# Two products of a recurrent scan, each split into two column halves of the matrix array

## The chip, the cores and the metric

The kernel runs on one core of one Trainium2 chip. A core has a matrix engine (TensorE, "PE" in the profile, with its weight loads shown apart as "PEld"), a vector engine (VectorE, DVE), a scalar engine (ScalarE, ACT), a general engine (GpSimd, POOL) and a queue engine that mostly starts transfers (SyncE, SP). The metric is the device time of one execution in microseconds, lower is better.

## The reference, cut to what matters

The kernel computes one layer of a bidirectional recurrent model on 128 context tokens and 2048 latent tokens of width 1024: a normalisation with modulation, one input projection, a mixer, an output projection. Half of the mixer's channels go through a gated short convolution. The other half, 8 heads of 64 channels, go through a delta-rule recurrence, once in each direction of time:

```
def step(S, inp):                       # S: (64 value x 64 key) per head
    r_t, w_t, k_t, v_t, kk_t, a_t = inp
    s_kk = einsum('bdhij,bdhj->bdhi', S, kk_t)
    S = S * w_t - s_kk x (kk_t * a_t) + v_t x k_t     # x: outer product
    return S, einsum('bdhij,bdhj->bdhi', S, r_t)
```

The states at the end of the context are an output as well, and the latent scans begin from cached states. All of it is in float32.

## The kernel before, in words

There are three phases: the input projection with everything that prepares the scan's operands (to about 1020 us of the span), the scan (about 1020 to 1590 us) and the output projection (from about 1525 us on, at first between the work of the scan).

The recurrence is cut into chunks of 64 tokens. A *unit* is one chunk of one pair of heads in one direction. A *stage* is two groups of 8 units, one group for each direction, and there are 17 stages (`stages`, L800 to L804). For each unit the kernel turns the 64 steps into a few matrix products:

- `partM` (L871) makes the products `psF` and `psG` (L892) and the transposes `psQ` (L885), three stages ahead of use.
- `partI` (L909) inverts small triangular blocks on GpSimd, and `partU` (L981) joins the 32 by 32 blocks of the inverse with products `psU` (L992) and `psW` (L999) on 32 by 32 tiles of the array.
- `partB` (L1011) applies the inverse, `psX` (L1018), which ScalarE copies into the operand tiles `stl` and `str`; and then makes the *operator* product `psE` (L1029), one for each unit and head: `g.lt` as weights (128 rows by 128 columns), `g.rt` as moving operand (128 rows by 128 columns). VectorE masks it into `E` (L1030).
- `partS` (L1034) walks through the 8 units of each group one after another. For each unit and head the *state* product `psS` (L1054) has `E` as weights (128 by 128) and `sv` as moving operand (128 rows by 64 columns: the state above, the values below). Its first 64 rows are the next state, which VectorE scales into the next unit's `sv` (L1067); its last 64 rows are the output (`outputs`, L1075), read by VectorE or ScalarE every fourth unit.

So the state product of a unit waits for VectorE's scaling after the one before it, in two chains (one for each direction), and all other products are there to be done between the links. The order in which the program emits the work is written out by hand (`ORDER`, L688, and the loop in `main`, L1172 to L1217). The framework's scheduler then orders the instructions of each engine by its own simulated timeline (L1409); the matrix engine's queue as it stands in the trace isn't the order of emission, but its own mixture of it. PSUM has 2 buffers for `partM` (`O.pm`), 2 for `psX`, `psE`, `psU`, `psW` and `psT` together (`O.p2`) and 4 for `psS` (`O.pS`).

A float32 product is two pairs of a weight load and a matmul in the profile: 17 stages with 2 groups of 16 products each are 544 products `psE`, and stand there as x1088; `psS` likewise.

Two products elsewhere are made on parts of the array already: `psU`/`psW`, which alternate between two 32 by 32 tiles, and `mod_rows` (L186 to L190), where four products, each with 128 rows by 32 columns of weights, write to the partitions 0, 32, 64 and 96 of one PSUM tile.

Of the kernel before, what the change touches and what calls it, by code (L numbers as in the profile page):

```python
# [690 lines left out]
def phase2(K):  # L691
    nc, tc, A, S = K.nc, K.tc, K.A, K.S
    V, G, P, T = nc.vector, nc.gpsimd, nc.scalar, nc.tensor
# [78 lines left out]
    def copy(k, dst, src, negate=False):  # L772
        if negate:
            if k in ON_DVE:
                V.tensor_scalar(dst, src, -1.0, None, ALU.mult)
            else:
                P.activation(dst, src, AF.Copy, scale=-1.0)  # L777
        else:
            (V.tensor_copy if k in ON_DVE else P.copy)(dst, src)  # L779
# [16 lines left out]
    def tl(shape, tag, b, pool=None, dt=F32):  # L796
        return (pool or O.l0).tile(shape, dt, tag=tag, name=f"{tag}_{K.u()}", bufs=b)
# [29 lines left out]
    H0, H1, FULL = slice(0, 64), slice(64, 128), slice(0, 128)  # L827
# [20 lines left out]
    def half(g, n):  # L848

        h = n if g.d == 0 else 1 - n  # L850
        return slice(h * 4, h * 4 + 4)
# [159 lines left out]
    def partB(s, st):  # L1011
        for n in range(2):
            for gi, g in enumerate(st.g):
                us = half(g, n)
                g.E.append(tl([128, 4, 2, 128], "E", 4))
                px = O.p2.tile([128, 4, 128], F32, tag="s", name=f"psX{s}_{gi}_{n}")
                for i in range(4):
                    T.matmul(px[:, i, :], B.zb[:, gi, us.start + i, :], g.F[:, us.start + i, :], start=True, stop=True)  # L1018
                for hd in range(2):
                    copy("x" if hd else "y", g.fs[64:128, :, hd, us], px[64 - hd * 64:128 - hd * 64].rearrange("p u (b t) -> p b u t", b=2), True)  # L1020
            yield
            for h2 in range(2):
                for gi, g in enumerate(st.g):
                    us = half(g, n)
                    k = (h2 if g.d == 0 else 1 - h2) * 2
                    pe = O.p2.tile([128, 2, 2, 128], F32, tag="s", name=f"psE{s}_{gi}_{n}{h2}")
                    for i in range(2):
                        for hd in range(2):
                            T.matmul(pe[:, i, hd, :].rearrange("p (b t) -> p b t", b=2), g.lt[:, :, hd, us.start + k + i].rearrange("p b t -> p (b t)"), g.rt[:, :, hd, us.start + k + i], start=True, stop=True)  # L1029
                    V.tensor_tensor(g.E[n][:, k:k + 2].rearrange("p a b c -> p (a b) c"), pe[:].rearrange("p a b c -> p (a b) c"),  # L1030
                                    B.msk[:, ME[g.d]].unsqueeze(1).broadcast_to((128, 4, 128)), ALU.mult)
                yield

    def partS(s, st, nxt):  # L1034

        sp = {}
        for i in range(8):
            for gi, g in enumerate(st.g):
                d = g.d
                ctx = g.blk is None  # L1040
                u = i % 4 * 2 + i // 4 if ctx else i
                u = u if d == 0 else 7 - u
                p, c = g.units[u]
                lastc = c == ((1 if d == 0 else 0) if ctx else (33 if d == 0 else 2))
                sv = g.sv
                n, k = (u // 4 if d == 0 else 1 - u // 4), u % 4

                m, q = (u % 2, u // 2) if ctx else (u // 4, u % 4)
                if i == 0 and not ctx and gi in held:
                    G.tensor_copy(sv[0:64, u], held.pop(gi)[:])  # L1050
                if i % 4 == 0:
                    sp[gi] = O.pS.tile([128, 4, 2, 64], F32, tag="S", name=f"psS{s}_{gi}_{i}")
                for hd in range(2):
                    T.matmul(sp[gi][:, q, hd, :], g.E[n][:, k, hd, :], sv[:, u, hd, :], start=True, stop=True)  # L1054
                if not (lastc and not ctx):
                    if ctx and lastc:
                        so = tl([64, 2, 64], "so", 2)
                        dst = so[:]
                    elif (not ctx) and i == 7:
                        if nxt.g[gi].blk is None:  # L1060
                            held[gi] = tl([64, 2, 64], "held", 2)
                            dst = held[gi][:]
                        else:
                            dst = nxt.g[gi].sv[0:64, 0 if d == 0 else 7]
                    else:
                        dst = sv[0:64, u + (1 if d == 0 else -1)]
                    r = V.tensor_tensor(dst, sp[gi][0:64, q], B.pc[0:64, d, 2 * p:2 * p + 2, c:c + 1].broadcast_to((64, 2, 64)), ALU.mult)  # L1067
                    O.scaled = r.ins
                    if ctx and lastc:
                        D(S["nst"][:, d, 2 * p:2 * p + 2, :], so[:])  # L1070
                if i % 4 == 3:
                    outputs(g.units[0][0], g.blk, m, sp[gi])
            yield

    def outputs(p, blk, m, ps):  # L1075

        y, there = ynew.setdefault((p, blk), (None, []))
        if y is None:
            y = tl([128, 4, 128], "y", 5)
            ynew[p, blk] = y, there  # L1080
        r = slice(m * 64, m * 64 + 64)
        src = ps[64:128].rearrange("p q h v -> p q (h v)")
        if m in there:
            V.tensor_tensor(y[r], src, y[r], ALU.add)
        else:
            copy("o", y[r], src)
        there.append(m)
        if len(there) == 4:
            ynew.pop((p, blk))
            pend.append(finish(p, blk, y))  # L1090
# [68 lines left out]
    def main():  # L1159
# [5 lines left out]
        sts[LA] = partL(LA)  # L1165
        run(partU(0, sts[0]))
        bb = partB(0, sts[0])
        next(W)
        for _ in range(3):
            next(bb)  # L1170
        tail = iter(())
        for s in range(NST):  # L1172
            st = sts.pop(s)
            more = s + 1 < NST
            W = partW(s + 1, sts[s + 1]) if more else iter(())
            uu = partU(s + 1, sts[s + 1]) if more else iter(())
            own, bb = bb, partB(s + 1, sts[s + 1]) if more else iter(())
            gens = dict(L=W, b=own, U=uu, B=bb)

# [23 lines left out]
            for i, _ in enumerate(partS(s, st, sts.get(s + 1))):  # L1203
                for _ in range((2, 2, 2, 1, 1, 0, 0, 0)[i]):
                    next(m, None)
                next(tail, None)
                if s < NST - 1:
                    emit(i + 1)
                for f in todo[:1] if s < NST - 3 else todo:
                    next(f, None)  # L1210
# [203 lines left out]
```

## Time and profile before

| what | value |
|---|---|
| median of 3 runs | 1759.63 us (1756.57, 1759.63, 1762.25) |
| span of the profiled execution, first to last instruction | 1752.9 us |
| what the median has beside that span | 6.7 us |
| PE busy / PEld busy | 1647.9 us (94%) / 1558.8 us (89%) |
| DVE / ACT / POOL busy | 1093.0 us (62%) / 870.1 us (50%) / 582.1 us (33%) |
| mean granted TensorE clock | 0.972 |

The profile gives the profiled execution's own time as this span; what stands beside it is start and end of the execution. A row of the timeline is "start us, duration us, engine, line, operation, out<-in, shapes, xcount", with the idle time before it in brackets; the shape of a matmul or weight load begins with rows\*columns of the weights. Successive instructions of a line are merged into one row. The end of a matmul is modelled: it lies some 0.17 us behind the moment at which the array could take the next, so the pace within a row of n matmuls is (duration of the row - duration of one) / (n - 1).

### The profile page before, as it was taken

The page shows a single profiled execution, that of the slowest core. Times are in us where ns is not written, and L with a number is a line of the kernel's source. Part 1 is how long each engine was busy: PE and PEld are TensorE (multiplying, and loading weights), DVE is VectorE, ACT ScalarE, POOL GpSimd, SP SyncE. Part 2 cuts the span into 40 slices and gives each one's busy share as a digit, 9 for nine tenths or more (in the row PEclk, how much of TensorE's full clock was granted, in tenths as well). Part 3 has the DMA queues.
Part 4 walks back from the last instruction along what each step waited for, and adds up shares of the span by engine and source line. Part 5 has one row for each costly group of instructions (what it writes and reads, how often), then busy time and mean ns, then how long its engine had stood idle before and what let it go on. Part 6 is the DMA issues. An engine that isn't in the chain of part 4 may idle for free. (4 is left out here: it accounts for less than half of the span.)

```text
span 1752.9 us, 33041 instructions
## 1 busy us (share of the span) xinstructions
PE 1647.9 (94%) x12400; PEld 1558.8 (89%) x12400; DVE 1093.0 (62%) x2092; ACT 870.1 (50%) x1719; POOL 582.1 (33%) x1089
## 2 busy tenths in 40 slices
PE   5999899998999999999998989999999999899998
PEld 2889898998999998999998979899999999787886
DVE  5875788866567766567764544475776666656333
ACT  4534455534143433334442367687788787633222
POOL 0011111111011101011120587777777778223221
PEclk9899999999999999999999998899999999999999
DMA  9797778785557646477666585587677875746442
GB/s 367 208 234 220 233 241 246 232 255 151 148 160 227 169 147 174 135 258 217 195 214 225 173 196 135 141 192 187 174 198 189 191 185 120 180 151 206 151 144 90
DMA packets 315825, 335.69 MB, mean 192 GB/s; under 512 B 166985, under 2 KB 263881, under 8 KB 301585
## 3 DMA queue, kind: packets, MB, share of 16 engines
q1 hardware_dynamic: 243360, 324.52, 62.6%
q10 hardware_dynamic: 70944, 4.60, 2.9%
q0 software_dynamic: 1360, 4.46, 0.7%
q8 instruction: 98, 1.61, 0.4%
q14 instruction: 63, 0.51, 0.1%
HBM read 221.42 MB, written 112.08 MB: 190 GB/s over the span
## 5 line engine op out<-in xcount | busy, mean ns | idle before, releaser
L934 POOL TENSOR_TENSOR zt<-zt,ztmp 128x30 f32<-128x30 f32 (+7 forms) x510 | 197.3, 387 | 39.3
L1054 PE MATMUL psS<-sv,E 128*128 128x64 f32 x1088 | 155.1, 277 | 1.0 <-DVE sv L1067 0.6
L1029 PE MATMUL psE<-str,stl 128*128 128x128 f32 x1088 | 144.1, 281 | 11.3 <-DVE E L1030 7.0
L1054 PEld LDWEIGHTS psS<-sv,E 128*128 128x128 f32 x1088 | 145.4, 200 | 3.3 <-DVE sv L1067 0.8
L1029 PEld LDWEIGHTS psE<-str,stl 128*128 128x128 f32 x1088 | 131.8, 194 | 14.1 <-DVE E L1030 7.9
L931 POOL TENSOR_TENSOR ztmp<-ab,zt 128x60 f32<-128x60 f32 (+7 forms) x255 | 130.8, 513 | 19.2
L1067 DVE TENSOR_TENSOR sv<-psS,pc 64x128 f32<-64x128 f32 x254 | 69.2, 277 | 92.9 <-PE psS L1054 92.2
L779 ACT COPY bd<-rr 64x512 f32<-64x512 f32 x136 | 84.0, 617 | 75.7 <-DMA rr<-scr_ops 23.3
L323 POOL TENSOR_TENSOR shk<-rawl 128x384 f32<-128x384 f32 (+1 forms) x24 | 20.7, 861 | 291.9 <-ACT rawl L319 291.9
L1030 DVE TENSOR_TENSOR E<-psE,msk 128x512 f32<-128x512 f32 x136 | 92.7, 684 | 33.0 <-PE psE L1029 32.3
L892 PE MATMUL psF<-rr,bd 128*128 128x128 f32 x544 | 80.0, 295 | 16.2 <-ACT Q L779 9.8
L892 PEld LDWEIGHTS psF<-rr,bd 128*128 128x128 f32 x544 | 70.7, 203 | 20.4 <-ACT Q L779 12.9
L1350 POOL TENSOR_TENSOR z<-z,x 128x512 f32<-128x512 f32 x32 | 43.6, 1364 | 126.6 <-DVE z L1346 105.9
L1018 PE MATMUL psX<-F,zb 128*128 128x128 f32 x544 | 78.2, 297 | 3.2 <-ACT zb L777 2.3
L197 POOL TENSOR_TENSOR hslb<-kd,hshb 128x384 fp32r<-128x384 f32 (+1 forms) x24 | 26.7, 1113 | 164.0 <-ACT hshb L196 143.5
L160 PE MATMUL mmc<-h,w 128*128 128x384 f32 (+1 forms) x192 | 67.9, 354 | 13.4 <-ACT q1r L321 9.8
L323 POOL TENSOR_TENSOR shv<-rawl 128x384 f32<-128x384 f32 (+1 forms) x24 | 25.4, 1060 | 153.4 <-ACT rawl L319 153.4
L892 PE MATMUL psG<-rr,bd 128*128 128x128 f32 x544 | 72.0, 280 | 4.4 <-DVE F L893 4.4
L1018 PEld LDWEIGHTS psX<-F,zb 128*128 128x128 f32 x544 | 71.6, 209 | 4.0 <-POOL zt L934 1.9
L892 PEld LDWEIGHTS psG<-rr,bd 128*128 128x128 f32 x544 | 65.7, 193 | 5.0 <-DVE F L893 4.8
L161 PE MATMUL mmc<-h,w 128*128 128x384 f32 (+1 forms) x192 | 66.1, 344 | 0.0
L162 PE MATMUL mmc<-h,w 128*128 128x384 f32 (+1 forms) x192 | 65.7, 342 | 0.0
(307 smaller groups left out, 5205.4 us busy)
## 6 DMA issues: line engine op xcount, KB each, us to landing
w<-scr_wsp SPq DMA_DIRECT2D x68, 1024.0 KB, 7.3
scr_wsp<-w SPq DMA_DIRECT2D x34, 1024.0 KB, 6.0
rr<-scr_ops SPq DMA_DIRECT2D x64, 512.0 KB, 4.6
scr_ops<-sp SPq DMA_DIRECT2D x160, 192.0 KB, 5.2
wr<-in_win SPq DMA_DIRECT2D x34, 512.0 KB, 6.3
ab<-scr_at SPq DMA_DIRECT2D x34, 256.0 KB, 4.2
x<-in_x SPq DMA_DIRECT2D x17, 512.0 KB, 3.8
wadas<-in_wada SPq DMA_DIRECT2D x8, 1024.0 KB, 13.0
```

The costliest lines, as they stand in the source:

```text
L160: T.matmul(ps[:, :n], w[:, 0, k], hh[:, 0, k, :n], start=k == 0, stop=False)
L161: T.matmul(ps[:, :n], w[:, 0, k], hh[:, 1, k, :n], start=False, stop=False)
L162: T.matmul(ps[:, :n], w[:, 1, k], hh[:, 0, k, :n], start=False, stop=k == 7)
L779: (V.tensor_copy if k in ON_DVE else P.copy)(dst, src)
L892: T.matmul(ps[:, i, :].rearrange("p (a b) -> p a b", b=64), w[:, u, :], x[:, :, u, :], start=True, stop=True)
L931: G.tensor_tensor(tv, ab[:, j:j + 2, j + 2:32].unsqueeze(1).broadcast_to((128, kn, 2, n)), zt[:, :kn, j:j + 2].unsqueeze(3).broadcast_to(( ...
L934: G.tensor_tensor(zt[:, :kn, j + 2:32], zt[:, :kn, j + 2:32], tv[:, :, r], ALU.subtract)
L1018: T.matmul(px[:, i, :], B.zb[:, gi, us.start + i, :], g.F[:, us.start + i, :], start=True, stop=True)
L1029: T.matmul(pe[:, i, hd, :].rearrange("p (b t) -> p b t", b=2), g.lt[:, :, hd, us.start + k + i].rearrange("p b t -> p (b t)"), g.rt[:, :, ...
L1030: V.tensor_tensor(g.E[n][:, k:k + 2].rearrange("p a b c -> p (a b) c"), pe[:].rearrange("p a b c -> p (a b) c"), B.msk[:, ME[g.d]].unsquee ...
L1054: T.matmul(sp[gi][:, q, hd, :], g.E[n][:, k, hd, :], sv[:, u, hd, :], start=True, stop=True)
L1067: r = V.tensor_tensor(dst, sp[gi][0:64, q], B.pc[0:64, d, 2 * p:2 * p + 2, c:c + 1].broadcast_to((64, 2, 64)), ALU.mult)
```

## The change

Both products are issued as two halves. A half has all 128 rows, and 64 of the 128 columns, of the weights, and so writes 64 of the 128 output partitions; the moving operand of both halves is the same, and is streamed once for each. Nothing else is changed: the same PSUM tiles are read by the same instructions. `H0` and `H1` are the slices 0:64 and 64:128.

```
-  T.matmul(pe[:, i, hd, :].rearrange("p (b t) -> p b t", b=2),
-           g.lt[:, :, hd, us.start + k + i].rearrange("p b t -> p (b t)"),
-           g.rt[:, :, hd, us.start + k + i], start=True, stop=True)
+  for b, c in enumerate((H0, H1)):
+      T.matmul(pe[c, i, hd, :].rearrange("p (b t) -> p b t", b=2),
+               g.lt[:, b, hd, us.start + k + i],
+               g.rt[:, :, hd, us.start + k + i], start=True, stop=True)
...
   for hd in range(2):
-      T.matmul(sp[gi][:, q, hd, :], g.E[n][:, k, hd, :], sv[:, u, hd, :], start=True, stop=True)
+      for m_ in (H0, H1):
+          T.matmul(sp[gi][m_, q, hd, :], g.E[n][:, k, hd, m_], sv[:, u, hd, :], start=True, stop=True)
```

More of the change, by code (lines that the diff above doesn't have):

```diff
@@ L1028, in partB @@
                         for hd in range(2):
-                            T.matmul(pe[:, i, hd, :].rearrange("p (b t) -> p b t", b=2), g.lt[:, :, hd, us.start + k + i].rearrange("p b t -> p (b t)"), g.rt[:, :, hd, us.start + k + i], start=True, stop=True)
+                            for b, c in enumerate((H0, H1)):
+                                T.matmul(pe[c, i, hd, :].rearrange("p (b t) -> p b t", b=2), g.lt[:, b, hd, us.start + k + i], g.rt[:, :, hd, us.start + k + i], start=True, stop=True)
                     V.tensor_tensor(g.E[n][:, k:k + 2].rearrange("p a b c -> p (a b) c"), pe[:].rearrange("p a b c -> p (a b) c"),
```

## The prediction

> **What bounds the kernel now.** I read the page first, then the busy time by windows, then the two products' rows, and last the timeline of one stage.
>
> ```profile
> span 1752.9 us, 33041 instructions
> PE 1647.9 (94%) x12400; PEld 1558.8 (89%) x12400; DVE 1093.0 (62%) x2092; ACT 870.1 (50%) x1719; POOL 582.1 (33%) x1089
> ```
> ```profile
> 1300.00:1400.00 100.00, 96.35 (x1153) 93.65 (x1152) 64.54 (x134) 82.31 (x158) 76.77 (x172) 1.00 0.82 191
> ```
> ```profile
> PEld psF L892 <- ACT Q L779: 10.3, 18, 1.8
> PE psE L1029 <- DVE E L1030: 1.0, 1, 1.0
> PE psS L1054 <- DVE sv L1067: 0.6, 1, 0.6
> ```
>
> The second fence is 100 us from the middle of the scan (PE, PEld, DVE, ACT, POOL busy, then the clock): TensorE is busy for 96 of them, ScalarE, the next, for 82. The third is the chain of waits of TensorE and its loads from 1100 to 1500 us: in 400 us the longest sum is 10.3 us. So in the scan the time is the length of TensorE's own queue, and a microsecond put in or taken out there counts nearly whole. The state chain isn't the limit: its wait for VectorE is 0.6 us.
>
> ```profile
> L1054 PE MATMUL psS<-sv,E x1088: 218/275/475, 1034.2 to 1588.6; 128*128 128x64 f32 x182
> L1029 PE MATMUL psE<-str,stl x1088: 275/275/422, 1030.2 to 1566.6; 128*128 128x128 f32 x182
> 1249.21 1.87 PEld L1029 LDWEIGHTS psE<-str,stl 128*128 128x128 f32 x16
> 1249.32 1.95 PE L1029 MATMUL psE<-str,stl 128*128 128x128 f32 x16
> 1250.99 0.97 PEld L1054 LDWEIGHTS psS<-sv,E 128*128 128x128 f32 x8
> ```
>
> The rows of the two products give ns min/median/max, first and last start. The pace: psE (1.95 - 0.275) / 15 = 0.112 us a matmul, its loads (1.87 - 0.19) / 15 = 0.112; the loads of psS (0.97 - 0.19) / 7 = 0.111. The shortest psS lasts 218 ns, psE 275: 57 ns less, half a pace, for half as many moving columns (64, not 128). So psE is balanced (load and stream 0.11 each), while psS streams for some 0.055 and then stands until the next 128 columns of weights are in. psS wastes half its slot, and that is all a split into column halves could get.
>
> **The change part by part.**
>
> *Do column halves run side by side?* The trace has column tiles with all 128 rows in L190.
>
> ```profile
> 34.33 1.06 PE L190 MATMUL psrow<-wadas,scp 128*32 128x512 f32 x8
> 84.93 1.05 PE L190 MATMUL psgr<-wgate,scp 128*32 128x512 f32 x4
> 211.49 1.41 PE L190 MATMUL psgr<-wgate,scp 128*32 128x512 f32 x3
> 212.83 0.44 PE L160 MATMUL mmv<-h,w 128*128 128x384 f32 x1
> 213.11 0.34 PE L161 MATMUL mmv<-h,w 128*128 128x384 f32 x1
> ```
>
> At 211.49 three matmuls follow each other (another product held one of the two tiles): (1.41 - 0.59 for the last) / 2 = 0.41 us each. Yet four on two tiles take 1.05, and eight on four tiles 1.06: no more than two in a row, 0.82, and the modelled tail. The tiles run in parallel, though each has its own moving stream. Their loads do too: on one path four loads, each a quarter of 0.111, would have put the last tile 0.05 us later with four tiles than with two, and the rows differ by 0.01.
>
> *psE, 1088 records.* Each becomes two, side by side; each half still streams 128 columns. Estimate 0.112 us a pair, as now: nothing. Upper bound, no overlap: 0.224, +122 us. A lower bound under 0.112 is excluded, since the stream isn't shortened.
>
> *psS, 1088 records.* Each half loads 64 columns and streams 64. Bounds: half of 0.111 (0.056) below, no gain (0.112, if the loads share one path) above. The nearest row is the 32 by 32 tiles' psU, below: (1.20 - 0.19) / 63 = 0.016 a record, 0.032 for a record on each of two tiles, where a quarter of 0.111 is 0.028; 4 ns over. I take 0.058: 1088 x (0.1115 - 0.058) = 58.2 us less.
>
> *Changing the tiling.* Before, only the 32 by 32 products broke the row of whole-array work. Now every change between the two products and any other does.
>
> ```profile
> 1244.63 0.56 PE L1054 MATMUL psS<-sv,E 128*128 128x64 f32 x4
> 1245.02 0.44 PE L892 MATMUL psF<-rr,bd 128*128 128x128 f32 x2
> 1245.30 1.95 PE L1029 MATMUL psE<-str,stl 128*128 128x128 f32 x16
> 1247.08 0.56 PE L1054 MATMUL psS<-sv,E 128*128 128x64 f32 x4
> 1247.48 2.00 PE L892 MATMUL psG<-rr,bd 128*128 128x128 f32 x16
> ...
> 1251.10 1.00 PE L1054 MATMUL psS<-sv,E 128*128 128x64 f32 x8
> ...
> 1252.38 1.06 PE L892 MATMUL psF<-rr,bd 128*128 128x128 f32 x8
> 1253.37 1.20 PE L992 MATMUL psU<-zr,GA 32*32 32x32 f32 x64
> 1254.50 1.10 PE L1054 MATMUL psS<-sv,E 128*128 128x64 f32 x8
> 1255.44 1.11 PE L892 MATMUL psF<-rr,bd 128*128 128x128 f32 x8
> ...
> 1270.48 0.56 PE L1054 MATMUL psS<-sv,E 128*128 128x64 f32 x4
> 1270.87 1.11 PE L1018 MATMUL psX<-F,zb 128*128 128x128 f32 x8
> 1271.82 0.56 PE L1054 MATMUL psS<-sv,E 128*128 128x64 f32 x4
> 1272.57 0.38 PE L892 MATMUL psF<-rr,bd 128*128 128x128 f32 x1 [0.19 <-ACT Q L779]
> ```
>
> The price, from psF to psU to psS: the last of the 8 psF ends at 1252.38 + 1.06 = 1253.44 and so starts 0.275 earlier, at 1253.165; the next could start at 1253.28. psU starts at 1253.37: 0.09 us for nothing. Its weights, which are otherwise loaded under the matmul before, are loaded only then (mmv at 212.83 shows such a load as 0.10 us more than its neighbour: 0.44 against 0.34). The same at the way out: psU ends at 1254.57, its last starts 0.19 earlier at 1254.38, the next could start at 1254.40 or a little later, psS starts at 1254.50, and its eight take 1.10 where eight unbroken take 1.00 (the row at 1251.10). Counted over the whole, from the last psF (1253.165) to the last psS (1254.50 + 1.10 - 0.275 = 1255.325) it is 2.16 us; without breaks it would be 0.112 + 64 x 0.016 + 0.725 (eight unbroken psS, 1.00 - 0.275) = 1.86. So a way in and out costs 0.30 us with weights of 32 columns inside. With 64 columns the first load in is 0.027 longer: 0.33 us. Bounds: two bare drains, 0.19, below, if all loads are hidden; above, drains of 0.09 to 0.10 with loads of 0.055 in and 0.11 out, 0.36.
>
> The number: in the stage above, from 1242.96 to 1272.57, the two products form 11 runs (first psS at 1244.63, last at 1271.82), 9 of them with whole-array work on both sides. Counted through the scan, from the psE at 1030.2 to the psS at 1588.6, there are 178 runs, with 145 ways in from and 155 ways out to whole-array work. These 300 are new: 150 pairs x 0.33 = 49.5 us more. The other ways lead to and from the 32 by 32 products, which had their breaks already; 33 runs that follow one now load 64 columns, not 128: 33 x 0.055 = 1.8 us less.
>
> The Trainium skill, "TensorEngine Tiling (Array Packing)", section "Key Properties", states that a change of the tiling mode, not just of the tile, drains the engine. It gives no price; the 0.09 us ahead of psU and ahead of mmv agree with it, and if the rule didn't hold the sum would be 58 us less instead of 10.
>
> *The rest.* VectorE reads the same tiles with the same instructions. The number of loads and matmuls rises by 2176 each; psU's 0.016 us a record shows that the queue can issue at least twice as fast as the 0.029 that psS halves need. A state link gets shorter, which helps nothing while it is no limit. psF's waits for ACT (18, about one a stage; the row at 1272.57) come right behind two short psS runs, and a drain there is hidden in them: up to 0.2 us each, 3 us. Against that stands that the scheduler sets a new order for twice as many instructions, so that waits like the 10.3 us above can grow. I set both at nothing.
>
> *The sum*, against the profiled execution: -58.2 + 49.5 - 1.8 = -10.5 us, a span of 1742. The median of the runs lies 6.7 us above the profile's span, so 1759.6 - 10 = 1749.
>
> **The rivals.**
>
> *The switching costs more than psS saves* (slower). It decides at 60 us in all: 182 pairs at 0.33, or 0.40 us a pair. For it: a run of 4 psS, the commonest (the rows at 1244.63 and 1270.48), saves 4 x 0.0535 = 0.21 us and pays 0.33, so every cut more by the new order loses. Against it: the price is measured above and my upper bound is 0.36. At 200 pairs and 0.36 it is +12, at 220 and 0.40 it is +28: 1765 to 1788.
>
> *Loads of the two halves share one path.* psS stays at 0.112, psE too: +48, 1807. Against it stand the four tiles of L190.
>
> *The halves run one after another.* psE 0.224 (+122), psS 0.116 (+5), switches +48: +175, 1935. If besides no load runs under the other half's matmul, psE takes 2 x (0.056 + 0.107) = 0.326 and psS 2 x (0.056 + 0.055) = 0.222: +233 and +120, with the switches +400, 2160. The rows of L190 speak against both. The Trainium skill, "TensorE: Matmul & The Clock Gate", section "The mechanism", says that weight loads overlap matmuls in flight only where the row group differs; both halves use all rows, so by that rule it would be the last case. This trace doesn't agree: whole-array loads run under whole-array matmuls here (0.112 for both).
>
> *It comes out even.* The gain is given back in waits for ScalarE, which is busy for 82%, and the kernel stays within 5 us: 1755 to 1764. For it: the net is a difference of two numbers of about 50.
>
> *Fewer runs.* If the scheduler comes nearer to the order of emission, where I count 7 runs a stage, about 102 pairs are new: -60 + 34 = -26, 1733.
>
> **How the numbers follow.** The sum holds (-25 to -5 us) with 0.34, fewer runs 0.10, even 0.18, the switching outweighs 0.27, loads on one path 0.06, halves one after another 0.05. A measurement of this kernel tells some 0.3% (5 us) from no change; so faster 0.44, same 0.18, slower 0.38. The forecast is 1749, with 1735 to 1755 as its own range. The whole range goes from the fewest runs (1733, with the psS at its lower bound of 0.056 and 0.30 a pair: 1725) to the top of the slower case (1788, and a little of waits: 1790); what it leaves out are the last two cases, 0.11.
>
> **What would show it.** Right: psS records with 128\*64 weights at a pace of about 0.029 us over both halves, psE at 0.056; about 178 runs with 0.09 us idle or a long first matmul at each end; TensorE's busy time in the scan hardly smaller, with loads well below. Wrong: psE's union above 160 us (no overlap); psS's loads still 0.11 for two halves; many more than 180 runs. The granted clock could upset it too:
>
> ```profile
> 1221.28 2.08 PE L892 MATMUL psF<-rr,bd 128*128 128x128 f32 x8 [1.46 <-ACT Q L779]
> ```
> ```profile
> 1200.00:1230.00 30.00, 28.17 (x315) 0.85 0.80 186
> ```
>
> After that wait of 1.46 us the eight psF take 2.08 us instead of 1.06, and the granted clock of these 30 us is 0.85. If the bubbles of switching bring such stretches more often, each costs about 0.15 x 30 = 4.5 us.

## The result and the profile after

The changed kernel is slower by a little: 1768.99 us in the median of 14 runs against 1762.33 for the kernel before beside it. The ratio is 1.0041, with a 95% interval of 1.0021 to 1.0061. The forecast was 1749 us, with 1735 to 1755 as its own range. The time lies inside the whole range that the prediction gave (1725 to 1790), but on the other side of the kernel before.

The page of the changed kernel, its first lines (span, busy time and share of each engine):

```profile
span 1769.6 us, 37328 instructions
PE 1638.3 (93%) x14576; PEld 1515.4 (86%) x14576; DVE 1091.6 (62%) x2092; ACT 867.0 (49%) x1719; POOL 585.2 (33%) x1089
```

The two products in the changed kernel (ns min/median/max, first and last start), and its timeline in the middle of the scan (start, duration):

```profile
L1056 PE MATMUL psS<-sv,E x2176: 218/222/371, 1045.4 to 1604.6; 128*64 128x64 f32 x198
L1030 PE MATMUL psE<-str,stl x2176: 272/273/476, 1041.5 to 1583.3; 128*64 128x128 f32 x198
```
```profile
1342.11 1.92 PE L1030 MATMUL psE<-str,stl 128*64 128x128 f32 x32
1343.86 0.40 PE L1056 MATMUL psS<-sv,E 128*64 128x64 f32 x8
1344.19 0.71 PE L892 MATMUL psF<-rr,bd 128*128 128x128 f32 x4
1344.74 0.83 PE L892 MATMUL psG<-rr,bd 128*128 128x128 f32 x6
1345.50 1.09 PE L1030 MATMUL psE<-str,stl 128*64 128x128 f32 x16
1346.52 0.49 PE L892 MATMUL psG<-rr,bd 128*128 128x128 f32 x2
1346.94 1.09 PE L1030 MATMUL psE<-str,stl 128*64 128x128 f32 x16
1347.97 1.16 PE L892 MATMUL psG<-rr,bd 128*128 128x128 f32 x8
...
1350.56 0.56 PE L1056 MATMUL psS<-sv,E 128*64 128x64 f32 x10
```

The reader sees that the halves do run side by side. 32 psE halves take 1.92 us, so the pace is (1.92 - 0.273) / 31 = 0.053 us a half; over all such rows it is 0.0547, or 0.109 for what was one record at 0.1117. Over all rows of psS it is 0.0292 a half, 0.058 a pair. The change of tiling also costs what was forecast. From the last of the two psG (start 1346.52 + 0.49 - 0.275 = 1346.735) to the last of the eight behind the 16 halves (1347.97 + 1.16 - 0.275 = 1348.855) it is 2.12 us; unbroken it would be 0.112 + 16 x 0.0547 + 7 x 0.112 = 1.77, so a way in and out costs 0.35 us. Laid out over the scan, the way in costs 0.143 and the way out 0.198.

Next, the scan as a whole. In the windows view of TensorE (start:end, us, PE busy, granted clock, DMA share, GB/s) the scan goes from the first psE to the last psS. First the kernel before, then the changed one:

```profile
1030.20:1588.60 558.40, 531.35 (x5940) 0.95 0.69 171
```
```profile
1041.50:1604.60 563.10, 518.67 (x8115) 0.95 0.68 170
```

The two profiled spans differ by 16.7 us, more than the medians (6.7). Of that, 11.3 us lie ahead of the scan, which the change doesn't touch; kernels below whose work ahead of the scan is the same begin it anywhere from 1032 to 1050 us, so I count this part as scatter of one execution. (The 6.7 us by which the median of before lies above its profiled span are mostly such scatter too: in the other profiled executions the time is only 1.7 to 2.2 us above the span.) In the scan the difference is 4.7 us.

What TensorE does in the scan can be laid out from the timeline: records times their pace ("own work"), changes of tiling times their price (0.143 and 0.198; 0.12 to 0.15 where 32 by 32 tiles are entered), and the rest, which is waits and time lost at half clock. The prices are means over many changes, so that a few us of the last column can be theirs. This table is worked out that way, for the two kernels and for those of the experiments below (the relief kernels and changed_short are left out of it):

| kernel | scan | own work | changes of tiling | waits and slow clock |
|---|---|---|---|---|
| before | 558.4 | 482.6 | 15.3 (96 changes) | 60.6 |
| after | 563.1 | 422.1 | 66.7 (406) | 74.3 |
| halves_old_order | 544.2 | 422.1 | 64.6 (394) | 57.6 |
| halves_fixed | 559.4 | 422.1 | 64.6 | 72.8 |
| whole_new_fixed | 550.2 | 482.6 | 12.7 (80) | 54.9 |
| e_only | 566.7 | 480.0 | 46.3 (277) | 40.4 |
| s_only | 556.5 | 424.5 | 75.6 (458) | 56.3 |
| all_halves | 605.6 | 437.3 | 21.4 (154) | 147.1 |
| all_halves_fixed | 554.2 | 437.3 | 15.0 (108) | 102.0 |
| whole_short | 535.2 | 482.6 | 15.3 | 37.4 |
| halves_short | 537.2 | 422.1 | 64.6 | 50.6 |
| all_halves_short | 532.0 | 437.3 | 15.0 | 79.8 |
| whole_free | 521.8 | 482.6 | 15.3 | 24.0 |
| halves_free | 526.8 | 422.1 | 64.6 | 40.2 |
| all_halves_free | 526.0 | 437.3 | 15.0 | 73.8 |

The first two rows hold the result. The own work fell by 60.5 us (1088 x 0.0532 for psS, 1088 x 0.0024 for psE), the changes of tiling rose by 51.4, so TensorE has 9 us less to do. And the scan isn't shorter: the waits and the slow clock took 14 us more. The clock has no part in that, since it is 0.95 in both views; what TensorE stands idle rose from 27.1 us (558.40 - 531.35) to 44.4 (563.10 - 518.67). The waits of TensorE's loads in the changed kernel from 1100 to 1500 us, against 10.3 for the longest sum before:

```profile
PEld psW L999 <- ACT bu L779: 8.3, 7, 3.5
PEld psE L1030 <- DVE E L1031: 7.2, 4, 5.2
PEld psF L892 <- ACT Q L779: 5.1, 8, 1.0
PEld psE L1030 <- ACT str L777: 3.4, 4, 1.7
```

The waits are no longer one row but several, for ScalarE and for VectorE. The question for the runs was why: the new order, the price of switching, or something that holds the scan from outside TensorE.

### The profile page after: what moved, and what is told of

Same layout as the page of the kernel before. It is cut to its first block, busy times and chain, and to the rows that moved or that the text cites. A ratio compares the mean times of both kernels' runs of the same rounds, so it can differ in the third digit from the quotient of the medians.

```text
span 1769.6 us, 37328 instructions
## 1 busy us (share of the span) xinstructions
PE 1638.3 (93%) x14576; PEld 1515.4 (86%) x14576; DVE 1091.6 (62%) x2092; ACT 867.0 (49%) x1719; POOL 585.2 (33%) x1089
## 5 line engine op out<-in xcount | busy, mean ns | idle before, releaser
L1030 PE MATMUL psE<-str,stl 128*64 128x128 f32 x2176 | 149.7, 286 | 21.5 <-DVE E L1031 13.9
L1030 PEld LDWEIGHTS psE<-str,stl 128*64 128x64 f32 x2176 | 123.6, 143 | 32.3 <-DVE E L1031 15.2
L1056 PE MATMUL psS<-sv,E 128*64 128x64 f32 x2176 | 109.9, 232 | 0.9 <-DVE sv L1069 0.8
L1056 PEld LDWEIGHTS psS<-sv,E 128*64 128x64 f32 x2176 | 88.1, 140 | 18.4 <-issue 4.5
L1069 DVE TENSOR_TENSOR sv<-psS,pc 64x128 f32<-64x128 f32 x254 | 66.0, 276 | 53.6 <-PE psS L1056 51.4
L892 PE MATMUL psG<-rr,bd 128*128 128x128 f32 x544 | 81.4, 292 | 4.0 <-DVE F L893 4.0
L160 PE MATMUL mmc<-h,w 128*128 128x384 f32 (+1 forms) x192 | 69.8, 363 | 15.5 <-ACT q1r L321 11.9
L1018 PEld LDWEIGHTS psX<-F,zb 128*128 128x128 f32 x544 | 67.7, 200 | 9.0 <-POOL zt L934 2.8
L161 PE MATMUL mmc<-h,w 128*128 128x384 f32 (+1 forms) x192 | 67.4, 351 | 0.0
L162 PE MATMUL mmc<-h,w 128*128 128x384 f32 (+1 forms) x192 | 67.3, 350 | 0.0
## 6 DMA issues: line engine op xcount, KB each, us to landing
wadas<-in_wada SPq DMA_DIRECT2D x8, 1024.0 KB, 12.6
```

The lines of the kernel that those rows point to most:

```text
L160: T.matmul(ps[:, :n], w[:, 0, k], hh[:, 0, k, :n], start=k == 0, stop=False)
L161: T.matmul(ps[:, :n], w[:, 0, k], hh[:, 1, k, :n], start=False, stop=False)
L162: T.matmul(ps[:, :n], w[:, 1, k], hh[:, 0, k, :n], start=False, stop=k == 7)
L892: T.matmul(ps[:, i, :].rearrange("p (a b) -> p a b", b=64), w[:, u, :], x[:, :, u, :], start=True, stop=True)
L1030: T.matmul(pe[c, i, hd, :].rearrange("p (b t) -> p b t", b=2), g.lt[:, b, hd, us.start + k + i], g.rt[:, :, hd, us.start + k + i], start=T ...
L1056: T.matmul(sp[gi][m_, q, hd, :], g.E[n][:, k, hd, m_], sv[:, u, hd, :], start=True, stop=True)
```

## The experiments

The ratios are to the kernel before, run beside each on the same chip, with their 95% intervals.

**One hunk each.** *e_only* has the first hunk of the change alone (psE in halves), *s_only* the second (psS).

```
e_only:  for b, c in enumerate((H0, H1)): T.matmul(pe[c, i, hd, :]..., g.lt[:, b, hd, ...], ...)    # psS whole
s_only:  for m_ in (H0, H1): T.matmul(sp[gi][m_, q, hd, :], g.E[n][:, k, hd, m_], ...)               # psE whole
```

> Only the operator product psE in halves, psS whole. psE gains next to nothing (0.1093 instead of 0.1117 us a pair, -2.6 us), and there are 277 instead of 96 changes of tiling, priced at +31 us. Theory (the price of a change is what counts): 25 to 30 us over the kernel before, and up to 10 more if the new order brings waits. Rival (changes are hidden in waits): within 5 us of before.

> Only the state product psS in halves, psE whole. psS gains 58 us; the runs are shorter, 458 instead of 96 changes of tiling, priced at +60 us. Theory: 0 to 10 us over the kernel before. Rival (the halves of psS gain nothing): 50 to 60 us over.

Measured: e_only 1769.87 us, 1.0063 (1.0038 to 1.0088); s_only 1758.95 us, 1.0004 (0.9984 to 1.0025). For e_only the table gives 28 us more of TensorE's time (own work -2.6, switching +31), yet its scan is longer by 8 only: the waits shrank by 20. The time is 11 us over before (0.63%), neither the 25 to 30 of the theory nor the rival's 5. So waits take up most of what is put into TensorE's queue, in this direction as well. For s_only the own work falls by 58 us and the switching rises by 60; it comes out even, in the table and in the time.

**The old order of TensorE.** *halves_old_order* has the whole change, and TensorE's instructions of the scan and the output projection are held to the order that the kernel before had in its queue, by dependencies that only fix an order. The other engines are ordered by the scheduler.

```
+for a, b in zip(flat, flat[1:]):      # TensorE's instructions, as before's scheduler had put them
+    tc.add_manual_dep(b, a.name, mybir.DependencyInfo(NoSync, DATA), reason="order")
```

> The changed kernel, with TensorE's instructions of the scan and the output projection tied to the order in which they stood before (the scheduler may not move them against each other; the two halves of a product stand together). Theory (the new order made the extra waits): pace -60 us and 394 instead of 96 changes of tiling, +49 us, without the 14 us of new waits and slow clock: about 11 us under the kernel before. Rival (the waits come from the halves themselves, whatever the order): as the changed kernel, about 7 us over the kernel before.

Measured: 1753.34 us, 0.9969 (0.9951 to 0.9987). That looked like an answer: with the order of before, the change gains 0.3%, and the new order costs the rest. The next two kernels show that it isn't.

**Both orders, on all engines.** *halves_fixed* is the change in the order of before, now fixed on all five engines; *whole_new_fixed* is the opposite, whole products in the order of the changed kernel.

```
+for e, words in ORDERS.items():       # TensorE, VectorE, ScalarE, GpSimd, SyncE
+    ...                               # flat: the instructions of e, in that order
     for a, b in zip(flat, flat[1:]):
         tc.add_manual_dep(b, a.name, mybir.DependencyInfo(NoSync, DATA), reason="order")
```

> The changed kernel with the instructions of all five engines, in the scan and the output projection, tied to the order in which they stood before; nothing differs from the kernel before but the halves. Theory (the halves gain 60 us of pace and pay 49 us of switching, the rest of the changed kernel's loss is the new order): 6 to 14 us under the kernel before. Rival (the order of the other engines is what matters): further from before than halves_old_order (0.9969 of it) by more than 5 us.

> The kernel before, its products whole, with the instructions of all five engines tied to the order of the changed kernel. Theory (the new order costs about 14 us by itself): 8 to 18 us over the kernel before. Rival (the order is harmless to whole products, and only the halves fit it badly): within 4 us of before.

Measured: halves_fixed 1763.07 us, 1.0016 (0.9998 to 1.0034); whole_new_fixed 1759.66 us, 1.0000 (0.9980 to 1.0019). The new order by itself costs nothing. And halves_fixed has the same TensorE queue as halves_old_order, instruction for instruction, so that the 0.5% between the two come from the other engines' order. Their scans, halves_old_order first:

```profile
1038.70:1582.90 544.20, 507.69 (x8116) 0.97 0.70 176
```
```profile
1035.40:1594.70 559.30, 514.57 (x8113) 0.96 0.69 171
```

The same 8116 matmuls (three records are missing in the second) take 15 us more. A kernel whose time TensorE's queue set could not do that. My theory of the order was dropped here.

**More halves, and no switching.** In *all_halves* the other products of the scan (psF, psG, psX, psQ, psT) are halves too, so that only the 32 by 32 tiles still change the tiling. *all_halves_fixed* is the same in the order of before.

```
-T.matmul(ps[:, i, :]..., w[:, u, :], x[:, :, u, :], start=True, stop=True)
+for c in (H0, H1):
+    T.matmul(ps[c, i, :]..., w[:, u, c], x[:, :, u, :], start=True, stop=True)
...   # psX, and the transposes psQ and psT as products with the identity, alike
```

The transposes cost more that way: in the scan psQ and psT have 688 records in place of 172, which is why the own work of these kernels is above that of the changed kernel in the table.

> All products of the scan that are 128 columns wide in halves: psF, psG, psX and the transposes psQ and psT (as products with the identity) as well as psE and psS. 154 changes of tiling are left, nearly all to and from the 32 by 32 products, priced at 6 us over the 96 of before. Theory (the changes of tiling ate the gain): the 58 us of psS and some 5 us of pace come back, less what other engines then hold up: 30 to 58 us under the kernel before. Rival (waits for ScalarE and VectorE bound the scan as soon as TensorE is quicker): no more than 10 us under before.

> All 128-column products of the scan in halves, as in all_halves, with the instructions of all five engines tied to the order of before. 108 changes of tiling are left, 0.3 us less in all than the 96 of before cost; pace -60 us for psS and psE and some -4 for the others. Theory (all_halves lost by its order alone, psE waiting for ScalarE's copies behind other work): 35 to 60 us under the kernel before. Rival (a quicker TensorE only waits for ScalarE and VectorE, whatever the order): no more than 15 us under.

Measured: all_halves 1821.37 us, 1.0348 (1.0318 to 1.0377); all_halves_fixed 1768.07 us, 1.0050 (1.0028 to 1.0072). In all_halves the scheduler's order put psE ahead of its operands. The waits of its loads from 1100 to 1500 us, and a row of its timeline:

```profile
PEld psE L1033 <- ACT str L777: 38.8, 13, 10.7
```
```profile
1331.23 1.98 PE L1033 MATMUL psE<-str,stl 128*64 128x128 f32 x16 [10.48 <-ACT str L777]
```

That is a cost of one order, so all_halves_fixed is the fairer test (the order is still one that was made for whole products). It has 46 us less of TensorE's time than the kernel before (452.3 against 497.9 with the changes), takes none of the switching that the change brought, and is still 0.5% slower. Its scan, and the waits of its loads from 1040 to 1590 us (L168 is the line of a helper through which all instructions of this kernel go):

```profile
1042.10:1596.20 554.10, 495.75 (x10030) 0.95 0.70 173
```
```profile
PEld psF L168 <- ACT Q L168: 24.2, 24, 2.6
PEld psE L168 <- DVE E L168: 12.6, 12, 4.6
PEld psE L168 <- ACT stl L168: 11.5, 8, 2.6
PEld psS L168 <- DVE sv L168: 3.5, 6, 1.3
```

So "the switching ate the gain" doesn't explain the result: without it the gain isn't there either. The waits hold it, mostly for ScalarE's copies (Q, stl).

**ScalarE relieved.** If ScalarE held the scan, moving copies from it to VectorE (busy 62%) should free it. *whole_relief*, *halves_relief* and *all_halves_relief* move the copies zb<-zc and the lower half of bd<-rr; *all_halves_relief_c* moves the second kind only. The order is that of before for all but the moved copies, whose place among VectorE's instructions is left to the scheduler.

```
+if k in ON_DVE:                                           # ON_DVE = "zc"; relief_c: "c"
+    nc.vector.tensor_copy(dst, src)                       # not in the fixed order
+else: P.copy(dst, src)
```

> The kernel before, whole products, all engines in the order of before, but six of ScalarE's copies a group of a stage go to VectorE (zb<-zc, and the lower half of each bd<-rr: 8 a stage in all, some 5 us of ScalarE a stage). Theory (ScalarE and TensorE bound the stage in turn, ScalarE in an unbroken row of copies of some 19 us): ScalarE's stretch gets shorter, TensorE, with some 28 us of its own a stage, takes over at once: 5 to 20 us under the kernel before. Rival (TensorE alone bounds): within 5 us of before.

> The changed kernel in the order of before, with the same copies moved to VectorE. TensorE's own sum is 10 us under that of before. Theory: 10 us further down than whole_relief. Rival (the halves gain nothing whatever bounds): as whole_relief within 4 us.

> All 128-column products of the scan in halves, all engines in the order of before, with the same copies moved to VectorE. TensorE's own sum is 46 us under that of before. Theory (all_halves_fixed gained nothing because TensorE waited for ScalarE): 25 to 55 us under the kernel before. Rival (something else holds the stage at 29.6 us: VectorE, GpSimd's inversion, the state chain): no more than 10 us under whole_relief.

> As all_halves_relief, but only the lower half of each bd<-rr goes to VectorE (4 copies a stage, 2.5 us of ScalarE). Theory: between all_halves_fixed (1.005 of before) and all_halves_relief, about half way. Rival (VectorE is hurt by what it takes over): better than all_halves_relief.

Measured, in this order: 1.0035 (1.0011 to 1.0060), 1.0052 (1.0024 to 1.0081), 1.0088 (1.0056 to 1.0121), 1.0061 (1.0039 to 1.0083). None got faster. The waits of all_halves_relief, from 1040 to 1590 us again, show why moving is no test of freeing: the wait for Q falls from 24.2 to 14.7, and VectorE's two grow from 16.1 (E 12.6, sv 3.5) to 30.1.

```profile
PEld psE L168 <- DVE E L168: 16.3, 12, 6.6
PEld psF L168 <- ACT Q L168: 14.7, 16, 2.2
PEld psS L168 <- DVE sv L168: 13.8, 13, 5.7
```

So these runs neither show nor exclude ScalarE as the bound: what they freed can't be told apart from the price paid on VectorE.

**GpSimd shortened.** I had not looked at GpSimd's timeline so far, since it is busy for 77 us of 100. The kernel before, one stage of it:

```profile
1261.97 0.20 POOL L923 COPY dgp<-ab 128x16 f32<-128x16 f32 x1 [0.36 <-DMA ab<-scr_at]
...
1287.37 0.60 POOL L934 TENSOR_TENSOR zt<-zt,ztmp 128x30 f32<-128x30 f32 x2
1288.27 0.62 POOL L935 DMA_DIRECT2D scr_zt<-zt  x1 [0.30 <-POOL zt L934]
1291.82 0.20 POOL L923 COPY dgp<-ab 128x16 f32<-128x16 f32 x1 [2.94 <-DMA ab<-scr_at]
```

From 1261.97 to 1287.97 the inversion is one chain of dependent instructions, each with a small gap to the next; then it writes its result and waits for the next stage's blocks, and starts again 29.85 us after it had started. A stage of the scan is 558 / 17 = 33 us on the average and, in the steady part, hardly longer than that chain. So I left part of the inversion out: the *_short* kernels leave out the last 6 of its 15 rounds (the blocks aren't fully inverted), in the order of before; *changed_short* is the change in its own order.

```
 for m in range(15):
+    if m >= 9: continue
```

> Whole products in the order of before; GpSimd's inversion leaves out the last 6 of its 15 rounds (the inverse, and so the result, is not the reference's), about 8 of its 27 us a stage. Theory (GpSimd's row of 27 us and the 3 us of transfers around it hold the stage at 29.6 us): the stage goes down to TensorE's own sum of some 28 us: 15 to 35 us under the kernel before. Rival (GpSimd is off the limit): within 5 us of before.

> The changed kernel in the order of before, with the same rounds of the inversion left out. TensorE's own sum is 10 us under that of whole products. Theory: 8 to 20 us under whole_short. Rival (halves gain nothing whatever bounds): within 4 us of whole_short.

> All 128-column products of the scan in halves in the order of before, with the same rounds left out. TensorE's own sum is 46 us under that of whole products. Theory: 25 to 50 us under whole_short. Rival (ScalarE or VectorE hold it then): within 10 us of whole_short.

> The changed kernel with all engines in its own order, with the same rounds left out. Theory: under whole_short as halves_short is, less what its own order costs (12 more changes of tiling, 2 us, and its waits): 0 to 15 us under whole_short. Rival (its order is what makes it slow): over whole_short.

Measured: whole_short 1742.33 us, 0.9885 (0.9844 to 0.9926); halves_short 1744.99, 0.9896 (0.9858 to 0.9935); all_halves_short 1746.48, 0.9896 (0.9854 to 0.9939); changed_short 1750.52, 0.9933 (0.9908 to 0.9958). Work taken from an engine that is busy a third of the span makes the kernel 1.2% faster. The scan of whole_short, and the wait of GpSimd that appears from 1100 to 1480 us, by which it now stands idle for more than a third of that time:

```profile
1041.70:1576.90 535.20, 517.23 (x5942) 0.98 0.72 178
```
```profile
POOL dgp L168 <- DMA ab<-scr_at: 143.0, 13, 21.2
```

But the halves gain nothing beside the whole products here either: three kernels, whose TensorE time differs by up to 46 us, within some 4 us. The changed kernel in its own order, changed_short, comes out 8 us over whole_short, where its rival had put it. In all_halves_short the loads still wait for ScalarE in the same 380 us:

```profile
PEld psF L168 <- ACT Q L168: 21.1, 20, 2.3
```

**Both taken off.** The *_free* kernels are the _short ones that also leave out the two kinds of copies which the relief kernels had moved (their targets hold old data), in the order of before.

```
+if k in "zc": pass            # no zb<-zc, no lower half of bd<-rr
+else: P.copy(dst, src)
```

> Whole products in the order of before, with the last 6 of 15 rounds of GpSimd's inversion left out and with 8 of ScalarE's copies a stage left out (zb<-zc and the lower half of bd<-rr), some 5 us of ScalarE a stage; the result is not the reference's. Theory (TensorE, ScalarE and GpSimd hold the stage at 28 to 30 us each by itself): TensorE is left as the limit, with little wait: 0 to 15 us under whole_short. Rival (ScalarE is no limit): as whole_short within 4 us.

> The changed kernel in the order of before, with the same work of GpSimd and ScalarE left out. TensorE's own sum is 10 us under that of whole_free. Theory: 5 to 15 us under whole_free. Rival (TensorE isn't the limit here either): within 4 us of whole_free.

> All 128-column products of the scan in halves in the order of before, with the same work of GpSimd and ScalarE left out. TensorE's own sum is 46 us under that of whole_free. Theory (with the two other limits gone TensorE's time counts): 20 to 45 us under whole_free. Rival (a chain through VectorE and the states holds the stage): within 8 us of whole_free.

Measured: whole_free 1728.31 us, 0.9805 (0.9764 to 0.9846); halves_free 1733.18, 0.9846 (0.9805 to 0.9886); all_halves_free 1732.89, 0.9832 (0.9787 to 0.9877). The copies are worth some 0.8% on top of GpSimd's rounds. In whole_free TensorE is nearly what sets the time: own work and changes are 497.9 of 521.8. Its waits from 1100 to 1480 us are small, and 100 us from the middle of its scan (PE, PEld, DVE, ACT, POOL busy, then clock, DMA share and GB/s) are full:

```profile
PEld psE L168 <- DVE E L168: 2.0, 4, 0.8
PEld psF L168 <- ACT Q L168: 1.0, 2, 0.7
```
```profile
1300.00:1400.00 100.00, 99.93 (x1203) 98.48 (x1202) 71.11 (x147) 69.62 (x139) 59.24 (x129) 1.00 0.87 202
```

And here the halves, with TensorE's time shorter by 11 us (halves_free) and 46 us (all_halves_free), should have shown their gain. They didn't. The same views of all_halves_free:

```profile
PEld psF L168 <- ACT Q L168: 11.6, 13, 2.0
PEld psE L168 <- DVE E L168: 4.2, 8, 0.9
```
```profile
1300.00:1400.00 100.00, 93.55 (x2048) 89.41 (x2044) 63.25 (x134) 67.78 (x136) 55.49 (x120) 0.95 0.83 195
```

The waits are back, and the clock is down to 0.95. The profiled execution of whole_free was 8.2 us faster than its median and that of all_halves_free 7.5 us slower, so the table overstates the distance of the two; by the medians they are 4.6 us apart, in intervals that overlap. What stays is that 46 us of TensorE's time bought at most some 6 us (the ratios differ by +0.0027, give or take 0.006).

## Why the prediction was wrong

**The pace of the halves: right.** psS was put at 0.058 us for two halves and came to 0.0585, psE at 0.112 and came to 0.109. The reading of L190 (streams and loads of column tiles run in parallel) carried over to tiles of 64 columns. The Trainium skill, "TensorE: Matmul & The Clock Gate", section "The mechanism", would have loads overlap matmuls only where the row group differs; the two halves have the same rows, and 32 of them take 1.92 us, so the trace doesn't agree, as the prediction had assumed.

**The price of a change: right.** 0.33 us was forecast for a way in and out; 0.143 + 0.198 = 0.341 was measured, the way out the dearer one (there the first load has 128 columns, which would explain it). The Trainium skill, "TensorEngine Tiling (Array Packing)", section "Key Properties", says that a change of the tiling mode drains the engine; the trace agrees, with these two prices.

**The number of runs: near.** 178 were forecast, counted in the trace of before; the new order has 194, with 170 ways in from whole-array work and 157 out, against 300 together in the forecast. The sum for switching was +49.5 and came to +51.4. So the net of TensorE, forecast as -10.5 us, is -9.1. The signs that the prediction named for being right came, the paces of 0.029 and 0.055 us and some 180 runs, and the time still went the other way: they test the sum for TensorE, not whether that sum is the time. Two slips in the working bear on nothing: by its own terms the bottom of the whole range is 1728, not 1725 (-60.4 - 1.8 + 102 x 0.30), and 0.016 us against 0.029 is 1.8 times as fast, not twice.

**"So in the scan the time is the length of TensorE's own queue": wrong, and this is the step that failed.** The prediction took the 96 us of busy in 100 for a full queue, and a full queue for the only limit. Those 100 us were at full clock; over the whole scan TensorE is busy for 531.35 of 558.40 us (95%), but busy time counts half-clock stretches whole, and the modelled tail of 0.17 us ahead of every wait. Laid out by paces, the scan is 482.6 us of own work and 15.3 of switching: 11% of it was neither. And a queue that is nearly full can have rows of the same length beside it. Two others were found beside it: GpSimd's inversion (26 us of chain and a turn-round, 29.85 us from start to start in the stage shown) and ScalarE's copies with the chain psF <- Q. That they explain the loss in full isn't shown, since with both shortened the halves still gain nothing (all_halves_free). The prediction saw the second, as 10.3 us of waits, and called it small; the first it never looked at. The runs show it from the other side. Shortening GpSimd gives 1.2%, leaving ScalarE's copies out besides gives 2.0%, and taking 46 us out of TensorE gives nothing that could be measured, in three pairs of kernels out of three (all_halves_fixed 1.0050 beside before, all_halves_short 0.9896 beside whole_short 0.9885, all_halves_free 0.9832 beside whole_free 0.9805).

**"I set both at nothing": wrong as a consequence.** Waits and slow clock rose by 14 us in the profiled executions. That is not owed to the new order of TensorE (whole_new_fixed: 1.0000), nor to the old one kept (halves_fixed has 72.8, as much as the changed kernel's 74.3; halves_old_order, with 57.6, is the exception, taken up below). What the three pairs above show instead is that time taken out of TensorE comes back as waits.

**The rivals.** "It comes out even", given 0.18, came nearest to what happened, waits for ScalarE in place of the gain, though not to its breadth (VectorE's waits, and GpSimd's row), and at +6.7 us the time lies just beyond its band. "The switching costs more than psS saves" ends on the right side for a reason that isn't so: the switching cost 51 us, under the 60 from which it decides. That the time lies inside the whole range is luck of the same kind, since the upper part of that range stood for this rival.

**What stays open.** Why it is +0.4% and not zero: the change has been run in three orders, at 0.9969, 1.0016 and 1.0041, so that the place of a few copies on other engines decides as much as the change does. Only halves_old_order beat the kernel before, and since halves_fixed didn't, with the same queue of TensorE, I don't credit the halves with it. Which chain holds all_halves_free, with GpSimd and ScalarE both shortened, wasn't settled either; the waits left are for ScalarE's Q and for VectorE's E, and the slow clock that follows them is a large part. A lead that no run followed: from 1100 to 1480 us ScalarE itself waits there for a transfer, the load of rr, for 20.1 us in all and up to 5.8 at a time; in whole_free that wait is 0.4 us.

```profile
ACT bd L168 <- DMA rr<-scr_ops: 20.1, 7, 5.8
```

The transfers were shortened in no run, and the engines that make them are busy for 0.83 (all_halves_free) and 0.87 (whole_free) of the 100 us shown above. And all three pairs go by the order of before, which was made for whole products. The orders that the scheduler made for halves were no better (changed_short, and all_halves with psE ahead of its operands), but a good one for all_halves wasn't tried, and no run ties the kernel before to its own order as a check on the tying itself. So that a better order, or quicker transfers, would bring out part of the gain isn't excluded.

## What to carry to other kernels

A busy share of 95% doesn't say that an engine alone sets the time: count its records, multiply them by the pace within unbroken rows, and see what is left over; here 11% of the scan was, and 28 us of added work (e_only) cost the scan only 8. Then look for other rows that are unbroken for nearly a whole stage, on engines of a low busy share above all, since GpSimd's dependent instructions with small gaps held a stage here at 77%. Splitting weights into column halves does what it promises for products whose load is longer than their stream (0.112 to 0.058 us here), but with other shapes in between it pays 0.34 us each time, and here it was worth nothing, since TensorE's queue alone didn't set the time.

## What the runs showed of the hardware

**A wait of TensorE costs more than its length.** Most stretches at half clock begin behind waits of a microsecond or more, and they last 3.4, 6.8, 10.2 or 13.7 us in these traces. Not every such wait brings one: in the scan of the kernel before 5 of 8 did, and two stretches came behind shorter waits. In all_halves_fixed, its timeline and the granted clock of these 1.9 us:

```profile
1355.26 1.98 PE L168 MATMUL psF<-rr,bd 128*64 128x128 f32 x16 [2.48 <-ACT Q L168]
```
```profile
1355.20:1357.10 1.90, 1.84 (x16) 0.50 0.04 16
```

16 halves that take 1.09 us in the changed kernel's rows above take 1.98 after the wait. The mean clock of 0.95 over the scan of before amounts to some 50 us at half speed, 25 us lost; with whole_free's 0.99 it is a quarter of that. The reverse shows in e_only: with 28 us more for TensorE to do, waits and slow clock are the smallest of all kernels with the full work (40.4). The Trainium skill, "TensorE: Matmul & The Clock Gate", section "What's actually happening", puts the fall to half speed after an idle window of about 3.4 us; here a wait of 1.46 us was enough (the prediction's last rows), while the multiples of 3.4 us agree.

**The order of the other engines moves this kernel by 0.5%** (0.9969 against 1.0016 with the same queue of TensorE), which is as large as the effect of the change.
